# Results of two head pairs turned later, own banks for the last piece, twelve warming products

## The chip, the cores and the metric

The kernel runs on one core of a Trainium2 chip. The metric is the device time of one execution in microseconds (us); lower is better. A kernel is judged by the median of several runs, and one further execution is recorded by the hardware profiler. TensorE (PE) multiplies into PSUM banks, VectorE (DVE) and ScalarE (ACT) read those banks and write the on-chip memory, GpSimd (POOL) fills constants, and SyncE (SP) issues most transfers. All weights are read from the chip's main memory during the run.

## The reference

A trunk of four layers over one sequence of 256 tokens, width 1024, in float32. Each layer is a token mixer and a squared-ReLU MLP, each behind an RMS norm and added to the residual stream. The mixers are, in order, differential attention, block-sparse attention, sliding-window attention, and differential attention again. Of the differential layer:

```python
qkv = h @ w_in
q, k, v = jnp.split(qkv, [DIFF_QK_WIDTH, 2 * DIFF_QK_WIDTH], axis=-1)
...
p = jax.nn.softmax(s, axis=-1)
p = p[:, :, 0] - lam * p[:, :, 1]
return jnp.einsum('bhqk,bkhe->bqhe', p.astype(v.dtype), v)
...
o = rms_norm(o, sub_g) * (1.0 - lambda_init)
return o.reshape(B, S, H * DIFF_V_DIM) @ w_out
```

It has 8 heads, each with a query and a key of two halves and a value 128 wide. The trunk ends in a last RMS norm:

```python
h = h + sqrelu_mlp(rms_norm(h, mlp_norm_g[i]), mlp_w_up[i], mlp_w_down[i])
return rms_norm(h, final_norm_g)
```

## The kernel before

**Numbers in two parts.** Every float32 product is made as three products of rounded parts: a high part, and a low part that holds the rest. Weights come in pieces of 128 x 2048 (`raw`), fetched by SP five pieces ahead. `stage` splits a piece: ScalarE writes `whi` (L80), VectorE writes `wlo` (L81), each in two halves, two pieces ahead of use; `whi` and `wlo` have three buffers each, so the L80 of a piece waits until TensorE has done with the piece three before. Activations are split the same way (`hg`, `oo`, `uu`).

**Order.** The text of the program is recorded in order, and a scheduler then moves independent instructions on each engine a little. Each engine works through its own queue.

**A differential layer** (`mixer_layer` with `mixer == 0`). Six projections of 512 columns follow each other, `order = (0, 1, "v", 2, "v", 3)`: four give queries and keys of two heads each, two give values. One projection is 48 products: 24 for the first 128 tokens, then 24 for the second (`proj`, L296, output `p_in`). Work of earlier heads is placed by hand between these products: `plan[2 * at]` runs between the two sets of 24, `plan[2 * at + 1]` behind the projection's evacuation (L586 for queries and keys, L581 for values, and the rotary embedding on VectorE, L304 to L309), and `plan[-1]` behind the last projection. The steps in a plan are:
- `QK(c)`: turn queries and keys of two heads (`p_qk`, L459) and split them.
- `SC(h)`: scores and softmax of head h (`p_s`, L271 to L273; L333, L336, L385).
- `TR(h)`: turn the weights of head h (`p_t`, L351) and evacuate them on ScalarE (`et`, L352).
- `AV(h)`: for odd h, multiply a pair of heads with the values (`p_av`, L357 to L359), take the norm of the result (L399 on ScalarE, L400 and the steps of `rsqrt` on VectorE) and write the scaled result `o` (L404 on VectorE).
- `OUT(g)`: turn the result of pair g, four transposes `p_o` (L409), and split it into `oo` (L411 on ScalarE, then L412 on VectorE).

Then `out_proj_all` multiplies with the output weights in four quarters g, one piece each (`p_d`, L271 to L273). Quarter g uses pair g's result. In the last quarter each block is added to the residual stream and split for the next norm (`into`: L622, L228, L229).

PSUM has eight banks of 512 columns in two rings of four: `acc` for `p_in`, `p_d` and `p_last`, and `wk` for the rest.

**The end** (`down_out`, last layer). The last down projection is made in two column pieces c of 512, for two sets of 128 tokens t, into banks `p_last`. `close` adds a bank to the residual (L702, VectorE) and sums its squares (L704, ScalarE); `finish` makes the factor of the last norm with short steps on VectorE (L710 to L717), scales the rows (L719 on ScalarE, L722 on VectorE) and sends them out (L720, L723). For the last piece and the last tokens (c = 1, t = 1) the second half of the sum is made 256 columns at a time: 12 products and `close` for the first 256, then 12 products in the other half of the same bank and `close`.

**The start.** `WARM` products of 128 x 128 ones (`p_warm`, L133) run on TensorE while the first data comes.

Of the kernel before, what the change touches and what calls it, by code (L numbers as in the profile page):

```python
# [11 lines left out]
F32 = mybir.dt.float32  # L12
F32R = mybir.dt.float32r
I32 = mybir.dt.int32
AF = mybir.ActivationFunctionType
OP = mybir.AluOpType
AX = mybir.AxisListType

P = 128
# [8 lines left out]
NEG = -1.0e38  # L28
LOOK = 2
FAR = 5  # L30
WARM = 11
RAW = 4


# [5 lines left out]
def trunk(ctx: ExitStack, tc: tile.TileContext, xT, gains, lams, swa_row, fng, weights, out):  # L40
# [8 lines left out]
    def bank(tag, name):  # L49
        return ps.tile([P, 512], F32, tag=tag, name=name, bufs=4)  # L50
# [427 lines left out]
    def mixer_layer(i, n):  # L478
        mixer, slot = i % 3, i // 3
        r = norm_factor(n)  # L480
        parts = []
# [43 lines left out]
        else:  # L525
# [43 lines left out]
                    [(TR, 4), (QK, 3), (OUT, 1), (SC, 6)], [(TR, 5), (SC, 7)],  # L569
                    [(AV, 4), (TR, 6), (AV, 5), (TR, 7), (AV, 6), (OUT, 2), (AV, 7), (OUT, 3)]]  # L570
            if mixer == 0:
                plan[8:] = [[(AV, 2), (QK, 2), (OUT, 0), (SC, 4)], [(AV, 3), (SC, 5)], [(TR, 4), (AV, 4), (OUT, 1)],
                            [(TR, 5), (AV, 5)],
                            [(QK, 3), (SC, 6), (SC, 7), (OUT, 2), (TR, 6), (AV, 6), (TR, 7), (AV, 7), (OUT, 3)]]
            for at, c in enumerate(order):
                p = proj(n, (512, 2), at == 0, [lambda do=do, x=x: do(x) for do, x in plan[2 * at]])
                if i == 0 and at == 0:
# [11 lines left out]
                    do(x)  # L589
            for do, x in plan[-1]:  # L590
                do(x)
            return parts
        for do in first + second:
            do()
        for _ in range(3):
            step()
        line.clear()
        return parts

# [22 lines left out]
        if b:  # L624
            norm_sum(n, j)

    def out_proj_all(parts, n):

        banks = [bank("acc", f"p_d{j}") for j in range(4)]
        for g in range(4):  # L630
            hi, lo = (r3(2)(x) for x in take())
            for d in range(8):
                p = banks[d // 2][:, S * (d % 2):S * (d % 2) + S]
                w = slice(P * d, P * d + P)
                for a in range(2):
                    x = parts[2 * g + a]
                    mm3(p, hi[:, a, w], lo[:, a, w], x[:, 0], x[:, 1], g + a + d % 2 == 0, g + a == 4,
                        skip_group_check=True)
                if g == 3:
                    into(n, d, p, None, True)  # L640

    def out_proj(parts, n):

        banks = [bank("acc", f"p_d{j}") for j in range(4)]
        two = [[r3(4)(x) for x in take()] for _ in range(2)]
        order = [(k, d) for k in range(6) for d in range(4)] + [(k, d) for d in range(4) for k in (6, 7)]
        for k, d in order:
            hi, lo = (x[:, k % 4, P * d:P * d + P] for x in two[k // 4])
            block_step(banks[d], hi, lo, parts[k], k == 0, k == 7)
            if k == 7:  # L650
                into(n, d, banks[d], None)
        for j in range(2):
            hi, lo = (r3(8)(x) for x in take())
            for b in range(2):
                p = bank("acc", f"p_e{b}")
                for k in range(8):
                    block_step(p, hi[:, k, P * b:P * b + P], lo[:, k, P * b:P * b + P], parts[k], k == 0, k == 7)
                into(n, 4 + 2 * j + b, p, None)
# [32 lines left out]
    def down_out(us, res, factor):  # L691

        grow = sb.tile([P, D], F32, tag="raw", name="grow", bufs=RAW)
        nc.sync.dma_start(grow, bcast(fng, D))
        ss = cst.tile([P, 4, NT], F32, name="fss")
        x = cst.tile([P, 2, NT], F32, name="fx")
        r = cst.tile([P, NT], F32, name="fr")

        def close(t, bank, c, part, first, width):

            y = res[t][:, 512 * c + first:512 * c + first + width]
            V.scalar_tensor_tensor(y, bank[:, first:first + width], factor[:, t:t + 1], y, op0=OP.mult, op1=OP.add)  # L702
            sq = sb.tile([P, 512], F32, tag="relu", name="sq")
            A.activation(sq[:, :width], y, AF.Square, accum_out=ss[:, part, t:t + 1])  # L704

        def finish(t, halves):

            o = slice(t, t + 1)
            last = x[:, 1, o]
            V.scalar_tensor_tensor(last, ss[:, halves, o], 0.5 / D, x[:, 0, o], op0=OP.mult, op1=OP.add)  # L710
            y, w = r[:, o], tiny.tile([P, 1], F32, tag="nw", name="nw", bufs=6)

            V.tensor_scalar(y.bitcast(I32), last.bitcast(I32), -0.5, 1597463007.0 - 2.0 ** 22 - 2.0 ** 31,
                            op0=OP.mult, op1=OP.add)
            for _ in range(3):
                V.scalar_tensor_tensor(w, y, y, last, op0=OP.mult, op1=OP.mult)
                V.scalar_tensor_tensor(y, w, 1.5, y, op0=OP.subtract, op1=OP.mult)  # L717
            rows = slice(P * t, P * t + P)
            A.activation(res[t][:, :512], res[t][:, :512], AF.Copy, scale=y)  # L719
            nc.scalar.dma_start(out[rows, :512], res[t][:, :512])  # L720
            for z in (slice(512, 768), slice(768, 1024)):
                V.scalar_tensor_tensor(res[t][:, z], res[t][:, z], y, grow[:, z], op0=OP.mult, op1=OP.mult)  # L722
                nc.sync.dma_start(out[rows, z], res[t][:, z])  # L723

        def sofar(t, parts):
            o = slice(t, t + 1)
            V.tensor_scalar(x[:, 0, o], ss[:, 0, o], 0.5 / D, 0.5 * EPS, op0=OP.mult, op1=OP.add)
            for j in parts:
                V.scalar_tensor_tensor(x[:, 0, o], ss[:, j, o], 0.5 / D, x[:, 0, o], op0=OP.mult, op1=OP.add)

        for c in range(2):
            banks = [bank("acc", "p_last") for _ in range(NT)]
            parts = []

            def last(t, ks, cols=slice(0, 512)):
                for q, k in ks:
                    hi, lo = parts[q]
                    u, s = us[4 * q + k], slice(P * t, P * t + P)
                    mm3(banks[t][:, cols], u[:, 0, s], u[:, 1, s], hi[:, k, cols], lo[:, k, cols],
                        q + k == 0, q + k == 10, skip_group_check=True)  # L740

            for q in range(8):
                parts.append([r3(4)(x) for x in take()])
                if q < 6:
                    for k in range(4):
                        for t in range(NT):
                            last(t, [(q, k)])
            ends = [(q, k) for q in (6, 7) for k in range(4)]
            last(0, ends)
            close(0, banks[0], c, c, 0, 512)  # L750
            if c == 0:
                last(1, ends)
                close(1, banks[1], 0, 0, 0, 512)
                for t in range(NT):
                    y = res[t][:, :512]
                    V.tensor_tensor(y, y, grow[:, :512], op=OP.mult)
                    sofar(t, [])
            else:
                finish(0, 1)
                last(1, ends[:4])  # L760
                for h in range(2):
                    last(1, ends[4:], slice(256 * h, 256 * h + 256))
                    close(1, banks[1], 1, 1 + h, 256 * h, 256)
                    if h == 0:
                        sofar(1, [1])
                finish(1, 2)
# [7 lines left out]
    for j in range(4):  # L774
        norm_sum(n, j)
    for i in range(DEPTH):
        parts = mixer_layer(i, n)
        n = new_norm(gv[:, 1, i, :])
        (out_proj if i % 3 == 1 else out_proj_all)(parts, n)
        held = {}  # L780

        def then(g):
            if i + 1 < DEPTH:
                if g == 1:
                    x = mean_row(n)
                    held["row"] = sb.tile([P, S], F32, tag="row", name="row", bufs=1)
                    V.reciprocal(held["row"], x)
            elif g == 1:
                held["factor"] = cst.tile([P, NT], F32, name="factor")
                V.reciprocal(held["factor"], mean_square(n))  # L790

                held["res"] = [room(16 + t, [P, D], f"res{t}") for t in range(NT)]
                for j in range(4):
                    p = bank("acc", "p_res")
                    for t in range(NT):
                        for b in range(2):
                            T.transpose(p[:, S * t + P * b:S * t + P * b + P],
                                        hT[j][:, S * b + P * t:S * b + P * t + P], ident)
                    for t in range(NT):
                        A.activation(held["res"][t][:, S * j:S * j + S], p[:, S * t:S * t + S], AF.Copy)  # L800

        us = up_proj(n, then)
        if i + 1 < DEPTH:
            n = new_norm(gv[:, 0, i + 1, :])
            down_proj(us, n, held["row"])
        else:
            down_out(us, held["res"], held["factor"])
# [78 lines left out]
```

## Time and profile before

| what | value |
|---|---|
| median of 3 runs | 1155.39 us (1154.45 to 1156.26) |
| profiled execution, its own time | 1154.87 us |
| its span, first to last instruction | 1152.8 us |
| granted TensorE clock, mean | 0.998 |
| transfers | 198.66 MB, mean 172 GB/s |
| p_o (L409) | 32 transposes in 8 groups |
| L411, ScalarE | 8 times, mean 681 ns |
| L412, VectorE | 8 times, mean 743 ns |
| p_warm (L133) | 22 records for 11 products |

A float32 transpose or warming product shows as one or two records of TensorE. A start-to-start distance on TensorE is surer than an end, since the ends of pipelined products are modelled. The page's engine shares are means over stages; what one wait is worth is read in its place in the timeline.

### The profile page before, as it was taken

The page shows a single profiled execution, that of the slowest core. Times are in us where ns is not written, and L with a number is a line of the kernel's source. Part 1 is how long each engine was busy: PE and PEld are TensorE (multiplying, and loading weights), DVE is VectorE, ACT ScalarE, POOL GpSimd, SP SyncE. Part 2 cuts the span into 40 slices and gives each one's busy share as a digit, 9 for nine tenths or more (in the row PEclk, how much of TensorE's full clock was granted, in tenths as well). Part 3 has the DMA queues.
Part 4 walks back from the last instruction along what each step waited for, and adds up shares of the span by engine and source line. Part 5 has one row for each costly group of instructions (what it writes and reads, how often), then busy time and mean ns, then how long its engine had stood idle before and what let it go on. Part 6 is the DMA issues. An engine that isn't in the chain of part 4 may idle for free.

```text
span 1152.8 us, 17102 instructions
## 1 busy us (share of the span) xinstructions
PE 1140.4 (99%) x6558; PEld 986.6 (86%) x6558; DVE 824.3 (72%) x1631; ACT 671.6 (58%) x1239; POOL 11.4 (1%) x39
## 2 busy tenths in 40 slices
PE   9999999999999999999999999999999999999997
PEld 7789888888887888888898888888888889888886
DVE  8978977656666698775568787775567788777453
ACT  6866655544476765654447866654447676665342
POOL 1000000000000000000000000000000000000000
PEclk9999999999999999999999999999999999999999
DMA  8543455555544355555564246555553434554551
GB/s 327 194 146 119 160 200 193 199 190 183 183 146 145 116 178 193 200 192 183 185 209 142 74 147 206 195 184 186 184 201 129 152 136 155 194 199 166 186 179 36
DMA packets 30608, 198.66 MB, mean 172 GB/s; under 512 B 3520, under 2 KB 5184, under 8 KB 7360
## 3 DMA queue, kind: packets, MB, share of 16 engines
q1 hardware_dynamic: 30240, 197.06, 49.6%
q8 instruction: 51, 0.84, 0.3%
q10 hardware_dynamic: 288, 0.52, 0.1%
q14 instruction: 29, 0.24, 0.1%
HBM read 196.52 MB, written 1.05 MB: 171 GB/s over the span
## 4 chain that ended last, share of the span: by engine, by line
PE 92%; DVE 3%; ACT 2%; DMA 2%; issue 1%; SPq 0%; DVEq 0%; ACTq 0%
PE p_up L603 20%; PE p_in L296 16%; PE p_down L603 15%; PE p_up L604 10%; PE p_down L604 8%; PE p_last L271 2%; PE p_last L273 2%; PE p_last L272 2%; PE p_d L273 2%; PE p_d L271 2%; DMA raw<-in_weights 2%; PE p_d L272 2%; PE p_av L434 1%; PE p_t L351 1%; PE p_s L271 1%; PE p_qk L459 1%
## 5 line engine op out<-in xcount | busy, mean ns | idle before, releaser
L81 DVE TENSOR_TENSOR wlo<-raw,whi 128x1024 fp32r<-128x1024 f32 (+1 forms) x374 | 447.1, 1209 | 202.9 <-ACT whi L80 201.9
L80 ACT ACTIVATE whi<-raw 128x1024 fp32r<-128x1024 f32 (+1 forms) x374 | 384.7, 1045 | 210.1 <-issue 111.1
L603 PE MATMUL p_up<-hg,whi 128*128 128x512 f32 x1024 | 356.9, 393 | 0.5 <-DVE hg L229 0.2
L604 PE MATMUL p_up<-hg,wlo 128*128 128x256 f32 x1024 | 284.9, 279 | 0.0
L603 PE MATMUL p_down<-uu,whi 128*128 128x512 f32 x768 | 266.4, 392 | 0.0
L603 PEld LDWEIGHTS p_up<-hg,whi 128*128 128x128 f32 x1024 | 191.5, 187 | 43.3 <-DVE hg L229 0.7
L604 PE MATMUL p_down<-uu,wlo 128*128 128x256 f32 x768 | 214.3, 279 | 0.0
L296 PE MATMUL p_in<-whi,hg 128*128 128x512 f32 (+1 forms) x736 | 212.9, 372 | 0.1
L604 PEld LDWEIGHTS p_up<-hg,wlo 128*128 128x128 f32 x1024 | 193.2, 189 | 0.5
L603 PEld LDWEIGHTS p_down<-uu,whi 128*128 128x128 f32 x768 | 143.7, 187 | 32.1
L296 PEld LDWEIGHTS p_in<-whi,hg 128*128 128x128 f32 x736 | 131.8, 188 | 24.7 <-issue 1.2
L604 PEld LDWEIGHTS p_down<-uu,wlo 128*128 128x128 f32 x768 | 144.8, 189 | 0.0
L296 PE MATMUL p_in<-wlo,hg 128*128 128x512 f32 (+1 forms) x368 | 130.3, 368 | 0.1
L676 ACT ACTIVATE uu<-u 128x512 fp32r<-128x512 f32 x64 | 40.5, 633 | 70.9 <-DVE u L674 70.9
L296 PEld LDWEIGHTS p_in<-wlo,hg 128*128 128x128 f32 x368 | 68.8, 188 | 12.1 <-DVE wlo L81 1.3
L609 ACT ACTIVATE cross<-p_up 128x256 f32<-128x256 f32 x128 | 48.1, 376 | 39.4 <-PE p_up L604 34.0
L228 ACT ACTIVATE hg<-hT,gn 128x256 fp32r<-128x256 f32 x64 | 31.6, 503 | 65.6 <-DVE hT L622 65.1
L336 ACT ACTIVATE e<-ns,nm 128x128 f32<-128x128 f32 (+1 forms) x128 | 56.8, 447 | 10.3 <-DVE nm L333 10.0
L677 DVE TENSOR_TENSOR uu<-u,uu 128x512 fp32r<-128x512 f32 x64 | 44.2, 691 | 21.5 <-ACT uu L676 21.5
L271 PE MATMUL p_d<-oo,whi 128*128 128x256 f32 x192 | 56.2, 293 | 0.0
L272 PE MATMUL p_d<-oo,whi 128*128 128x256 f32 x192 | 55.1, 287 | 0.0
L273 PE MATMUL p_d<-oo,wlo 128*128 128x256 f32 x192 | 54.7, 288 | 0.0
(182 smaller groups left out, 1262.1 us busy)
## 6 DMA issues: line engine op xcount, KB each, us to landing
raw<-in_weights SPq DMA_DIRECT2D x181, 1024.0 KB, 4.8
raw<-in_weights SPq DMA_DIRECT2D x8, 256.0 KB, 4.6
raw<-in_weights SPq DMA_DIRECT2D x4, 512.0 KB, 7.6
hT<-in_xT SPq DMA_DIRECT2D x8, 128.0 KB, 4.5
bias<-in_swa_row SPq DMA_DIRECT2D x1, 512.0 KB, 3.6
grow<-in_fng SPq DMA_DIRECT2D x1, 512.0 KB, 3.5
out<-res SPq DMA_DIRECT2D x4, 128.0 KB, 2.1
out<-res ACTq DMA_DIRECT2D x2, 256.0 KB, 2.2
```

The costliest lines, as they stand in the source:

```text
L80: A.activation(hi[:, s], raw[:, s], AF.Copy)
L81: V.tensor_tensor(lo[:, s], raw[:, s], f(hi[:, s]), op=OP.subtract)
L271: T.matmul(out, lh, rh, start=start, stop=False, **kw)
L272: T.matmul(out, lh, rl, start=False, stop=False, **kw)
L273: T.matmul(out, ll, rh, start=False, stop=stop, **kw)
L296: T.matmul(out[t], n.both[k // 2][:, k % 2, x, P * t:P * t + P], r3(kb)(parts[k // kb][w])[:, k % kb, :], start=fresh, stop=k == 7 and x + ...
L336: A.activation(e[:, s], ns[:, s], AF.Exp, bias=nm[:, t:t + 1], scale=-1.0, accum_out=l[:, t:t + 1])
L603: T.matmul(r3(2)(p), hi, x, start=start, stop=False, skip_group_check=True)
L604: T.matmul(p[:, :S], lo, x[:, 0], start=False, stop=stop, skip_group_check=True)
L609: A.activation(cross, p[:, S:], AF.Copy)
L676: A.activation(both[:, :, 0], r3(2)(u), AF.Copy)
L677: V.tensor_tensor(both[:, :, 1], r3(2)(u), f(both[:, :, 0]), op=OP.subtract)
```

## The change

`OUT(1)` moves from the middle of the last projection to behind it, ahead of `TR(5)`. `OUT(3)` leaves the plan and is handed to `out_proj_all` as `rest`, which calls it in the third quarter ahead of block 4. The other mixers hand over an empty step. In `down_out`, the second half of the last sum goes into banks of its own: the first half is closed by a 512-wide L702 without squares, and each 256 columns get a fresh bank. `WARM` becomes 12.

```diff
-WARM = 11
+WARM = 12
...
-                plan[8:] = [[(AV, 2), (QK, 2), (OUT, 0), (SC, 4)], [(AV, 3), (SC, 5)], [(TR, 4), (AV, 4), (OUT, 1)],
-                            [(TR, 5), (AV, 5)],
-                            [(QK, 3), (SC, 6), (SC, 7), (OUT, 2), (TR, 6), (AV, 6), (TR, 7), (AV, 7), (OUT, 3)]]
+                plan[8:] = [[(AV, 2), (QK, 2), (OUT, 0), (SC, 4)], [(AV, 3), (SC, 5)], [(TR, 4), (AV, 4)],
+                            [(OUT, 1), (TR, 5), (AV, 5)],
+                            [(QK, 3), (SC, 6), (SC, 7), (OUT, 2), (TR, 6), (AV, 6), (TR, 7), (AV, 7)]]
...
-            return parts
+            return parts, (lambda: OUT(3))
...
-    def out_proj_all(parts, n):
+    def out_proj_all(parts, n, rest):
...
             for d in range(8):
+                if (g, d) == (2, 4):
+                    rest()
...
-        def close(t, bank, c, part, first, width):
+        def close(t, p, c, part, first=0):
+            width = p.shape[-1]
             y = res[t][:, 512 * c + first:512 * c + first + width]
-            V.scalar_tensor_tensor(y, bank[:, first:first + width], factor[:, t:t + 1], y, op0=OP.mult, op1=OP.add)
-            sq = sb.tile([P, 512], F32, tag="relu", name="sq")
-            A.activation(sq[:, :width], y, AF.Square, accum_out=ss[:, part, t:t + 1])
+            V.scalar_tensor_tensor(y, p, factor[:, t:t + 1], y, op0=OP.mult, op1=OP.add)
+            if part is not None:
+                sq = sb.tile([P, 512], F32, tag="relu", name="sq")
+                A.activation(sq[:, :width], y, AF.Square, accum_out=ss[:, part, t:t + 1])
...
                 last(1, ends[:4])
+                close(1, banks[1], 1, None)
                 for h in range(2):
-                    last(1, ends[4:], slice(256 * h, 256 * h + 256))
-                    close(1, banks[1], 1, 1 + h, 256 * h, 256)
+                    p = bank("acc", "p_last")[:, :256]
+                    last(1, ends[4:], p, 256 * h, True)
+                    close(1, p, 1, 1 + h, 256 * h)
                     if h == 0:
                         sofar(1, [1])
```

More of the change, by code (lines that the diff above doesn't have):

```diff
@@ L597, in mixer_layer @@
         line.clear()
-        return parts
+        return parts, lambda: None
     def block_step(p, hi, lo, x, start, stop):
@@ L640, in out_proj_all, with out_proj @@
                     into(n, d, p, None, True)
-    def out_proj(parts, n):
+    def out_proj(parts, n, rest):
         banks = [bank("acc", f"p_d{j}") for j in range(4)]
@@ L733, in down_out, with last @@
             parts = []
-            def last(t, ks, cols=slice(0, 512)):
+            def last(t, ks, p=None, first=0, alone=False):
+                p = banks[t] if p is None else p
+                cols = slice(first, first + p.shape[-1])
                 for q, k in ks:
@@ L738, in last @@
                     u, s = us[4 * q + k], slice(P * t, P * t + P)
-                    mm3(banks[t][:, cols], u[:, 0, s], u[:, 1, s], hi[:, k, cols], lo[:, k, cols],
-                        q + k == 0, q + k == 10, skip_group_check=True)
+                    mm3(p, u[:, 0, s], u[:, 1, s], hi[:, k, cols], lo[:, k, cols],
+                        (q, k) == (ks[0] if alone else (0, 0)), (q, k) == ks[-1] and k == 3 and q > 5,
+                        skip_group_check=True)
             for q in range(8):
@@ L749, in down_out @@
             last(0, ends)
-            close(0, banks[0], c, c, 0, 512)
+            close(0, banks[0], c, c)
             if c == 0:
                 last(1, ends)
-                close(1, banks[1], 0, 0, 0, 512)
+                close(1, banks[1], 0, 0)
                 for t in range(NT):
@@ L776, in trunk @@
     for i in range(DEPTH):
-        parts = mixer_layer(i, n)
+        parts, rest = mixer_layer(i, n)
         n = new_norm(gv[:, 1, i, :])
-        (out_proj if i % 3 == 1 else out_proj_all)(parts, n)
+        (out_proj if i % 3 == 1 else out_proj_all)(parts, n, rest)
         held = {}
```

## The prediction

> **What bounds the kernel now.** I read the busy shares of the page first, then the chain that ended last, then the list of waits of TensorE alone, and last the timeline around the three places that the change touches. Columns of a timeline row: start in us, duration in us, engine, line, operation, output<-inputs, shape, count, and in brackets the idle time before it with what ended it.
>
> ```profile
> PE 1140.4 (99%) x6558; PEld 986.6 (86%) x6558; DVE 824.3 (72%) x1631; ACT 671.6 (58%) x1239; POOL 11.4 (1%) x39
> ...
> PE 92%; DVE 3%; ACT 2%; DMA 2%; issue 1%; SPq 0%; DVEq 0%; ACTq 0%
> ```
> ```profile
> PE p_o L409 <- DVE o L404: 1.5, 4, 0.5
> ...
> PE p_last L271 <- DVE res L702: 0.6, 1, 0.6
> ```
>
> TensorE is busy for 99% of the span and carries 92% of the last chain. So an edit on another engine is worth nothing unless it closes a hole in TensorE's stream or shortens what follows its last product. The waits name exactly two kinds of hole that this change aims at: four waits of the transposes p_o for the VectorE result o, and one of p_last for L702. The list counts idle time after modelled ends, so I size each hole from starts instead.
>
> **The second pair's result, OUT(1).** First diff layer; the second has the same rows 843.5 us later.
>
> ```profile
> 84.45 0.39 PE L296 MATMUL p_in<-wlo,hg 128*128 128x512 f32 x1
> ...
> 85.08 0.63 PE L409 MATMUL p_o<-ident,o 128*128 128x128 f32 x4 [0.24 <-DVE o L404]
> ...
> 85.46 0.70 PE L296 MATMUL p_in<-whi,hg 128*128 128x512 f32 x2
> ...
> 85.74 0.69 ACT L411 ACTIVATE oo<-p_o,gn 128x512 fp32r<-128x512 f32 x1 [1.28 <-PE p_o L409]
> ...
> 87.36 1.06 ACT L80 ACTIVATE whi<-raw 128x1024 fp32r<-128x1024 f32 x1 [0.93 <-PE p_in L296]
> ```
> ```profile
> 89.67 0.39 PE L296 MATMUL p_in<-whi,hg 128*128 128x512 f32 x1
> ...
> 89.90 0.49 PE L351 MATMUL p_t<-ident,e 128*128 128x128 f32 x3
> 90.10 0.69 ACT L586 ACTIVATE qk<-p_in,nr 128x512 f32<-128x512 f32 x1 [0.72 <-PE p_in L296]
> ...
> 90.68 0.48 ACT L352 ACTIVATE et<-p_t 128x384 f32<-128x384 f32 x1
> ...
> 90.81 0.36 PE L271 MATMUL p_d<-oo,whi 128*128 128x256 f32 x1
> ...
> 91.22 0.30 PEld L357 LDWEIGHTS p_av<-v,et 128*128 128x128 f32 x2 [0.24 <-ACT et L352]
> ...
> 91.68 0.42 DVE L309 TENSOR_TENSOR qk<-ropea,ropeb 128x256 f32<-128x256 f32 x1
> ```
> ```profile
> 92.23 1.04 PE L459 MATMUL p_qk<-ident,qk 128*128 128x128 f32 x8
> ```
> ```profile
> 928.62 0.63 PE L409 MATMUL p_o<-ident,o 128*128 128x128 f32 x4 [0.24 <-DVE o L404]
> ```
>
> One p_in product takes 0.23 us from start to start (89.67 to 89.90). From 84.45 to 85.08 pass 0.63, so the hole is 0.40. The built order of the changed kernel (which instruction follows which on each engine, without times) puts the four transposes 19 products later, behind the last product of the projection and ahead of p_t; o is long ready there. Without hole and transposes the next product comes at 84.45 + 0.23 = 84.68 instead of 85.46: the rest of the projection runs 0.78 earlier, its last product at 88.89. The transposes start at 89.12 and take their 0.38 (85.08 to 85.46), p_t starts at 89.50, and the first p_d 0.91 later (89.90 to 90.81), at 90.41.
>
> The new danger is on ScalarE. L411 now stands between the L586 that empties the projection and the L352 that the second half of p_av waits for, and p_av already waited for L352 before (0.24). L586 moves with the projection to 89.32. L411 follows 0.58 later (90.10 to 90.68) at 89.90; the transposes are out at 89.12 + 0.63, in time. L411 lasts 0.69, so L352 starts by 90.59 at the latest, about 90.5 if the next instruction overlaps it as L352 overlaps L586. It ends near 90.98 and p_av starts 0.06 later, as it did (90.68 + 0.48 to 91.22): 91.04. TensorE's own slot would be about 90.73 (two p_d now stand ahead of it, 0.20 and 0.12), so a wait of some 0.3 stays. Against 91.22 that is 0.18 earlier, and one p_d more, worth 0.12, is already done: **0.30 us per layer**.
>
> The same queue rule holds on VectorE: L412 (0.74, a row below) now stands ahead of the rotary sum L309. That makes L309 start at 91.68 - 0.78 + 0.74 = 91.64 at the latest and end at 92.06. p_qk has its slot 1.01 after p_av (91.22 to 92.23), at 92.05: nothing, or 0.05. The pair of L80 ahead of L586 is released by p_in (87.36), so it moves with the projection and does not hold L586.
>
> Ends for this term: best the whole hole, 0.40. Worst, L352 moves back by all of L411 and none of the 0.78 counts: 91.22 + 0.69 - 0.12, a loss of 0.57. I take 0.30, since each of its starts hangs on a TensorE row that does move.
>
> [...]
>
> **The last pair's result, OUT(3).** It moves from ahead of the output projection into its third quarter.
>
> ```profile
> 109.86 0.28 PE L271 MATMUL p_d<-oo,whi 128*128 128x256 f32 x1
> 109.98 0.28 PE L272 MATMUL p_d<-oo,whi 128*128 128x256 f32 x1
> 110.78 0.63 PE L409 MATMUL p_o<-ident,o 128*128 128x128 f32 x4 [0.52 <-DVE o L404]
> 111.16 0.36 PE L273 MATMUL p_d<-oo,wlo 128*128 128x256 f32 x1
> ```
> ```profile
> 111.49 0.67 ACT L411 ACTIVATE oo<-p_o,gn 128x512 fp32r<-128x512 f32 x1
> 116.47 2.01 ACT L80 ACTIVATE whi<-raw 128x1024 fp32r<-128x1024 f32 x2 [4.31 <-PE p_d L272]
> ```
> ```profile
> 112.95 0.74 DVE L412 SCALAR_TENSOR_TENSOR oo<-p_o,gn,oo 128x512 fp32r<-128x512 f32 x1
> ```
> ```profile
> 954.31 0.63 PE L409 MATMUL p_o<-ident,o 128*128 128x128 f32 x4 [0.52 <-DVE o L404]
> ```
>
> p_d products follow each other every 0.12; 0.80 pass before p_o, so the hole is 0.68. The built order shows 19 more p_d ahead of the transposes, 2.3 us, so o is there. A change of kind costs TensorE a little even without a wait; I leave 0.08 of the hole for it: **0.60 per layer**, ends 0.50 and 0.68. What is late next: the last quarter needs both halves of this result, 24 products (2.9 us) after the transposes end. From the start of p_o: 0.71 to L411 (110.78 to 111.49), 0.67, and 0.74 for L412, together 2.12, against 0.38 + 2.88 = 3.26. Cover 1.1 us, if L411 is ahead of the L80 pair, as the built order has it. The four transposes and their two evacuations are the same instructions as before, and neither SP's nor GpSimd's queue is passed.
>
> **The last piece.** The second 256 columns get a bank of their own, and a 512-wide L702 without a square closes the first half of the sum.
>
> ```profile
> 1141.46 0.39 PE L273 MATMUL p_last<-whi,uu 128*128 128x512 f32 x1
> ...
> 1142.24 0.16 DVE L717 SCALAR_TENSOR_TENSOR fr<-nw,fr 128x1 f32<-128x1 f32 x1
> ...
> 1142.43 0.88 DVE L722 SCALAR_TENSOR_TENSOR res<-res,fr,grow 128x256 f32<-128x256 f32 x2
> ...
> 1143.00 0.28 PE L273 MATMUL p_last<-whi,uu 128*128 128x256 f32 x1
> ...
> 1143.85 0.39 PE L271 MATMUL p_last<-whi,uu 128*128 128x256 f32 x1 [0.58 <-DVE res L702]
> ...
> 1145.27 0.28 PE L273 MATMUL p_last<-whi,uu 128*128 128x256 f32 x1
> 1145.58 0.48 DVE L702 SCALAR_TENSOR_TENSOR res<-p_last,factor,res 128x256 f32<-128x256 f32 x1 [1.05 <-PE p_last L273]
> ```
> ```profile
> 1139.17 0.75 DVE L702 SCALAR_TENSOR_TENSOR res<-p_last,factor,res 128x512 f32<-128x512 f32 x1 [7.43 <-PE p_last L273]
> ```
>
> Without the wait the second half's first product starts at 1143.00 + 0.12 and its last 11 steps of 0.12 later, at 1144.44 instead of 1145.27: 0.83 earlier. The new L702 (0.75) stands in VectorE's queue ahead of the final L717 of the first 128 rows. Its data is there (1141.46 + 0.39 = 1141.85), so it runs from 1142.24 and pushes L717, the L722 pair and its two output DMAs back 0.75: the pair ends at 1143.31 + 0.75 = 1144.06. The first 256-wide L702 (0.48) then runs to 1144.54 and VectorE is free 0.2 before the last L702, at 1144.44 + 0.28 + 0.03 = 1144.75. So those 0.75 lie beside TensorE's last products. After that the chain to the last DMA is the same. **0.83 us**; ends 0.5, if the 0.75 shows in part, and 0.83.
>
> **The twelfth warming product.**
>
> ```profile
> 1.00 4.58 PE L133 MATMUL p_warm<-ones 128*128 128x128 f32 x22 [1.00 <-POOL ones L124]
> ...
> 5.68 0.30 PEld L296 LDWEIGHTS p_in<-whi,hg 128*128 128x128 f32 x2 [0.29 <-ACT hg L228]
> ...
> 6.40 0.30 PEld L296 LDWEIGHTS p_in<-whi,hg 128*128 128x128 f32 x2 [0.43 <-DVE hg L229]
> ```
>
> One product is two records; 22 take 4.58, so two more take at most 0.42. The first real product waits for ScalarE's hg at 5.68 with 0.29 idle, the next pair again with 0.43 idle. These waits hide it: 0, at worst 0.13 (0.42 - 0.29) and then eaten by the next wait.
>
> **Sum.** 2 × 0.30 + 2 × 0.60 + 0.83 + 0 = 2.63 us. The profiled execution took 1154.87 us (span 1152.8, 2.07 around it) and would take 1152.24. The median of the three runs, 1155.39, lies 0.52 above it and becomes 1152.76, predicted 1152.8. With the low ends except the improbable loss (0 for OUT(1), 0.50, 0.5, -0.13) the gain is 1.4, with the high ends (0.40, 0.68, 0.83) 3.0.
>
> **The rivals.** First, the wait of OUT(1) only changes its name: p_av's wait for L352 grows as p_o's wait goes. It decides if L352 starts 0.3 us later than I place it, for instance because ScalarE is still in an L80 when the projection ends. For it: p_av waits there already. Against: L80 moves with p_in. Gain 2 × 0.60 + 0.83 = 2.03, time 1153.4.
>
> Second, the slower one: OUT(3) comes too late for the last quarter. Place: L411 behind the L80 pair at 116.47 rather than ahead of it. That pair waits for the end of the third quarter, would run from 115.87 to 117.88, and L411 and L412 to 119.29, where the last quarter's low half is wanted at about 115.7: 3.6 lost in each layer where 0.60 was gained. It decides as soon as the result is over 1.1 us later than above. For it: the pair is the next thing in that queue. Against: the built order. Time 1155.39 + 7.2 - 0.60 - 0.83 - 1.20 = 1160.0.
>
> Third, the change doesn't reach TensorE's order because the scheduler had already moved these transposes. The built order shows all four at new places, so I give this nothing.
>
> **How the numbers follow.** A difference under 0.2% (2.3 us, below 1153.1) is about what a measurement of this kernel can't tell from none; the three runs spread over 1.8 us. My forecast clears that bound by only 0.3 us, so its chance is 0.62, the first rival and other partial gains 0.29, the second and what else makes it slower 0.09. Of these come faster 0.62, same 0.29, slower 0.09. The range goes from the high ends of the terms with the runs' scatter below them, 1151.6, past the first rival to a gain that scatter nearly hides, 1154.9.
>
> **What would show it.** Right: p_o gone from TensorE's waits, p_av's wait on L352 still about 0.2 to 0.3 in each diff layer, no wait at p_last, the last p_last product 2.6 us earlier. Wrong: p_av waiting over 0.5, p_d waiting for L411 or L412 at the start of the last quarter, or the last 256-wide L702 waiting in VectorE's queue instead of for TensorE.

## The result

| | median | range | profiled execution, span |
|---|---|---|---|
| before | 1154.9 us (7 runs) | 1154.45 to 1156.26 | 1154.87, 1152.8 |
| after | 1151.68 us (7 runs) | 1151.44 to 1151.98 | 1151.98, 1149.9 |

The ratio is 0.9972, 95% interval 0.9962 to 0.9982. The change saves 3.2 us, 0.28%, where 2.63 us was forecast; the time lies inside the range, 0.08 above its lower end.

The page of the kernel after, busy shares and the chain that ended last, and then TensorE's whole list of waits (us in total, times, longest):

```profile
PE 1139.2 (99%) x6560; PEld 988.0 (86%) x6560; DVE 824.6 (72%) x1632; ACT 671.1 (58%) x1239; POOL 11.4 (1%) x39
...
PE 95%; DVE 2%; DMA 1%; ACT 1%; issue 0%; SPq 0%; DVEq 0%
```
```profile
PE p_warm L133 <- POOL ones L124: 1.0, 1, 1.0
PE p_qk L459 <- DVE qk L309: 0.7, 1, 0.7
PE p_s L271 <- issue: 0.6, 1, 0.6
PE p_in L296 <- DVE wlo L81: 0.3, 1, 0.3
PE p_up L603 <- DVE hg L229: 0.2, 1, 0.2
```

Both kinds of hole that the change aims at are gone: no p_o, no p_last. The last p_last product starts 2.87 us earlier (1145.27 before). TensorE now carries 95% of the last chain instead of 92%. The p_in wait of 0.3 is new but belongs to the start, where the first weights land at different moments: the first L80, which waits for them, starts at 4.59 in the kernel before and at 4.37 in after. It must be kept apart from the change, so I measure stages from start to start on TensorE. Rows of the kernel before (first p_o of the first differential layer, its first p_up, then p_sum and p_up at the two ends of the last layer's mixer), and the same of after:

```profile
68.27 0.60 PE L409 MATMUL p_o<-ident,o 128*128 128x128 f32 x4
...
120.45 0.50 PE L603 MATMUL p_up<-hg,whi 128*128 128x512 f32 x1
...
859.12 0.60 PE L249 MATMUL p_sum<-ones,acc 128*128 128x128 f32 x3
...
963.99 0.50 PE L603 MATMUL p_up<-hg,whi 128*128 128x512 f32 x1
```
```profile
68.55 0.60 PE L409 MATMUL p_o<-ident,o 128*128 128x128 f32 x4
...
119.60 0.50 PE L603 MATMUL p_up<-hg,whi 128*128 128x512 f32 x1
...
858.24 0.71 PE L249 MATMUL p_sum<-ones,acc 128*128 128x128 f32 x4
...
961.95 0.50 PE L603 MATMUL p_up<-hg,whi 128*128 128x512 f32 x1
...
1142.40 0.28 PE L273 MATMUL p_last<-whi,uu 128*128 128x256 f32 x1
```

Differences of these starts (worked out before rounding, so that a row can be 0.01 off), for these two kernels and for the parts of the change run alone (experiments below):

| kernel | first layer, p_o to p_up | last layer, p_sum to p_up | p_up to last p_last | last p_last to end of span |
|---|---|---|---|---|
| before | 52.18 | 104.86 | 181.28 | 7.49 |
| after | 51.05 | 103.71 | 180.45 | 7.48 |
| OUT(1) alone | 51.73 | 104.45 | 181.28 | 7.50 |
| OUT(3) alone | 51.47 | 104.22 | 181.28 | 7.49 |
| last piece alone | 52.19 | 104.86 | 180.45 | 7.49 |
| warming alone | 52.17 | 104.91 | 181.27 | 7.49 |

The change takes 1.13 and 1.15 us out of the two mixers and 0.83 out of the end: 3.11. The two profiled executions differ by only 2.89, because the one of after began its first p_o 0.28 later (68.55 against 68.27).

**OUT(1) after the change.** Timeline of the kernel after, where the last projection ends:

```profile
89.05 0.39 PE L296 MATMUL p_in<-whi,hg 128*128 128x512 f32 x1
...
89.28 0.60 PE L409 MATMUL p_o<-ident,o 128*128 128x128 f32 x4
...
89.71 0.49 PE L351 MATMUL p_t<-ident,e 128*128 128x128 f32 x3
...
90.06 0.68 ACT L411 ACTIVATE oo<-p_o,gn 128x512 fp32r<-128x512 f32 x1
...
90.63 0.49 ACT L352 ACTIVATE et<-p_t 128x384 f32<-128x384 f32 x1
...
91.17 0.30 PEld L357 LDWEIGHTS p_av<-v,et 128*128 128x128 f32 x2 [0.27 <-ACT et L352]
...
91.60 0.42 DVE L309 TENSOR_TENSOR qk<-ropea,ropeb 128x256 f32<-128x256 f32 x1
...
92.18 0.49 PE L459 MATMUL p_qk<-ident,qk 128*128 128x128 f32 x3
```

L352 starts as L411 ends, 0.57 after L411's start, and p_av waits for it (0.27, and again 0.27 in the last layer): the wait that the prediction kept is there. Whether a ready L352 could pass L411 is not shown: p_t is out at 90.20, when L411 has run since 90.06, so L352 had nothing to pass. On VectorE L309 starts at 91.60, as L412 (from 90.94, 0.75 long) ends, though its last input is out at 91.02 (L307). p_qk follows the product ahead of it (92.06) without a wait, as L309 is done at 92.02.

**OUT(3) after the change.** Timeline of the kernel after, third quarter of the output projection:

```profile
112.10 0.28 PE L273 MATMUL p_d<-oo,wlo 128*128 128x256 f32 x1
112.22 0.60 PE L409 MATMUL p_o<-ident,o 128*128 128x128 f32 x4
...
112.58 0.36 PE L271 MATMUL p_d<-oo,whi 128*128 128x256 f32 x1
...
112.78 0.28 PE L272 MATMUL p_d<-oo,whi 128*128 128x256 f32 x1
...
112.86 0.69 ACT L411 ACTIVATE oo<-p_o,gn 128x512 fp32r<-128x512 f32 x1 [1.43 <-PE p_o L409]
...
113.58 0.75 DVE L412 SCALAR_TENSOR_TENSOR oo<-p_o,gn,oo 128x512 fp32r<-128x512 f32 x1 [0.71 <-ACT oo L411]
```

p_o starts 0.12 after the p_d ahead of it, the plain step of such products, so nothing of the hole is left. The result is ready at 114.33; its low half is wanted by the 26th product after p_o, at about 112.58 + 0.08 + 25 × 0.12 = 115.66. The cover is 1.3 us.

**The end after the change.** Lines below L701 moved down by three to four: L705 and L721 are the L702 and L717 of before.

```profile
1140.09 0.74 DVE L705 SCALAR_TENSOR_TENSOR res<-p_last,factor,res 128x512 f32<-128x512 f32 x1
...
1140.75 0.15 DVE L721 SCALAR_TENSOR_TENSOR fr<-nw,fr 128x1 f32<-128x1 f32 x1
...
1141.73 0.48 DVE L705 SCALAR_TENSOR_TENSOR res<-p_last,factor,res 128x256 f32<-128x256 f32 x1
...
1142.71 0.48 DVE L705 SCALAR_TENSOR_TENSOR res<-p_last,factor,res 128x256 f32<-128x256 f32 x1 [0.50 <-PE p_last L273]
```

The last L705 waits 0.50 for TensorE, not for its queue. The added 512-wide L705 therefore lies wholly beside TensorE's last products.

### The profile page after: what moved, and what is told of

Read it like the earlier page. It is cut to its first block, busy times and chain, and to the rows that moved or that the text cites. A ratio compares the mean times of both kernels' runs of the same rounds, so it can differ in the third digit from the quotient of the medians.

```text
span 1149.9 us, 17106 instructions
## 1 busy us (share of the span) xinstructions
PE 1139.2 (99%) x6560; PEld 988.0 (86%) x6560; DVE 824.6 (72%) x1632; ACT 671.1 (58%) x1239; POOL 11.4 (1%) x39
## 4 chain that ended last, share of the span: by engine, by line
PE 95%; DVE 2%; DMA 1%; ACT 1%; issue 0%; SPq 0%; DVEq 0%
PE p_up L603 20%; PE p_in L296 18%; PE p_down L603 15%; PE p_up L604 11%; PE p_down L604 8%; PE p_last L273 3%; PE p_last L271 3%; PE p_last L272 3%; PE p_d L273 2%; PE p_d L271 2%; PE p_d L272 2%; PE p_t L351 1%; PE p_av L434 1%; PE p_s L271 1%; PE p_qk L459 1%; DVE wlo L81 1%
## 5 line engine op out<-in xcount | busy, mean ns | idle before, releaser
L81 DVE TENSOR_TENSOR wlo<-raw,whi 128x1024 fp32r<-128x1024 f32 (+1 forms) x374 | 447.3, 1209 | 205.5 <-ACT whi L80 204.5
L80 ACT ACTIVATE whi<-raw 128x1024 fp32r<-128x1024 f32 (+1 forms) x374 | 384.7, 1045 | 208.2 <-issue 111.1
L271 PE MATMUL p_d<-oo,whi 128*128 128x256 f32 x192 | 55.8, 291 | 0.0
L272 PE MATMUL p_d<-oo,whi 128*128 128x256 f32 x192 | 55.2, 288 | 0.0
```

What stands on the lines that cost most here:

```text
L80: A.activation(hi[:, s], raw[:, s], AF.Copy)
L81: V.tensor_tensor(lo[:, s], raw[:, s], f(hi[:, s]), op=OP.subtract)
L271: T.matmul(out, lh, rh, start=start, stop=False, **kw)
L272: T.matmul(out, lh, rl, start=False, stop=False, **kw)
```

## The experiments

**The four parts, each alone.** Each is the kernel before with one part of the change (the third was made from the kernel after by taking the other parts back).

OUT(1) alone:

```diff
-[(TR, 4), (AV, 4), (OUT, 1)], [(TR, 5), (AV, 5)],
+[(TR, 4), (AV, 4)], [(OUT, 1), (TR, 5), (AV, 5)],
```

> The kernel before with OUT(1) alone moved behind the last projection. Theory (the whole hole before p_o goes, one change between transposes and products goes with it, and p_av's wait on L352 stays at about 0.24): 0.45 us in each differential layer, 0.9 us in all, time ratio 0.9992. The prediction's own term would give 0.30 a layer, 0.6 us, ratio 0.9995. Rival (the wait only changes its name to p_av): under 0.2 us in all and a p_av wait over 0.5 us.

OUT(3) alone:

```diff
-[(QK, 3), ..., (TR, 7), (AV, 7), (OUT, 3)]]
+[(QK, 3), ..., (TR, 7), (AV, 7)]]
...
+                if (g, d) == (2, 4):
+                    rest()
```

> The kernel before with OUT(3) alone moved into the third quarter of the output projection. Theory: the whole hole of 0.68 us in each differential layer, 1.36 us, ratio 0.9988; no wait of p_d for L411 or L412. The prediction's term: 0.60 a layer, 1.2 us. Rival (the result is late for the last quarter): a wait at the first p_d of the last quarter and a gain under 1 us.

The last piece alone:

```diff
                 last(1, ends[:4])
+                close(1, banks[1], 1, None)
                 for h in range(2):
-                    last(1, ends[4:], slice(256 * h, 256 * h + 256))
-                    close(1, banks[1], 1, 1 + h, 256 * h, 256)
+                    p = bank("acc", "p_last")[:, :256]
+                    last(1, ends[4:], p, 256 * h, True)
+                    close(1, p, 1, 1 + h, 256 * h)
```

> The kernel before with the last piece's own banks alone. Theory: the last p_last product 0.83 us earlier, all of it kept up to the last transfer, ratio 0.9993. Rival (the extra 512-wide evacuation holds up VectorE's queue): the last 256-wide evacuation starts later than 0.03 us after TensorE's last product ends, and the gain is 0.5 us or less.

The twelfth product alone:

```diff
-WARM = 11
+WARM = 12
```

> The kernel before with twelve warming products alone. Theory: the extra product lies beside the wait for the first data, 0.0 us, ratio 1.0000 within 0.0005, and the runs scatter as those of the kernel before. Rival (the twelfth keeps the clock up or steadies the start): 0.3 us or more faster and a narrower scatter of the runs, which would account for the 0.3 us by which the medians differ more than the two profiles.

Measured beside the kernel before on the same chip (1154.99 us, 33 runs):

| part | median (11 runs each) | ratio and interval | saved, medians | saved, stages of the profile |
|---|---|---|---|---|
| OUT(1) | 1154.15 | 0.9993 [0.9984, 1.0002] | 0.84 | 0.45 + 0.41 |
| OUT(3) | 1153.69 | 0.9989 [0.9980, 0.9998] | 1.30 | 0.71 + 0.64 |
| last piece | 1154.18 | 0.9993 [0.9984, 1.0001] | 0.81 | 0.83 |
| warming | 1155.09 | 0.9998 [0.9989, 1.0007] | -0.10 | 0 |

One part by itself is at the edge of what the times resolve; only OUT(3) has an interval below one. The stage lengths resolve each, and the medians agree with them within 0.1 us. The parts add up: 2.95 by the medians without the warming (2.85 with it), 3.04 by the stages, against 3.2 and 3.11 for the whole. That they disturb one another does not show.

**After once more, as a measure for its neighbours.** The changed kernel, unaltered.

> The changed kernel once more, to compare the following with on one chip and to tell whether the gain of 3.2 us between the medians is more than the 3.1 us that the stages show (1.13 and 1.15 in the two differential layers, 0.83 at the end). Theory (stages alone, the rest is when the first weights land): 1151.9 us against 1155.0, ratio 0.9973, with p_o's first start between 68.2 and 69.6 us in any profile. Rival (the parts help each other): 1151.5 or less and a stage that is shorter than in the runs of single parts.

1152.04 us (1151.30 to 1153.01) against 1154.87 of before; ratio 0.9975 [0.9967, 0.9984]; stages 51.04, 103.74, 180.44. This is what the stages alone give. Only the band for the first p_o was too narrow: one of the profiles below has 67.98.

**Does the warming matter at all?** One product instead of twelve, in the changed kernel.

```diff
-    for _ in range(WARM):
+    for _ in range(1):
```

> The changed kernel with one warming product instead of twelve. Theory (the granted clock rises a fixed time after the first products and the first data hides most): the first projection runs at the lower clock until about 9 to 12 us, 0.5 to 2 us slower than the changed kernel. Rival (waits for data hide all of it): equal within 0.2 us, and the twelfth product can then not matter either.

1152.46 us (1151.82 to 1153.29), 0.42 above the run before, just under the 0.5 to 2 us that was expected. TensorE's waits of this kernel, and its first products in two stretches, followed by the same stretches of after (columns: length, busy time and count of TensorE, its weight loads, VectorE, ScalarE, GpSimd, granted clock, share of the transfer engines, GB/s):

```profile
PE p_in L296 <- ACT hg L228: 3.9, 1, 3.9
```
```profile
8.00:11.40 3.40, 3.40 (x9) 2.64 (x8) 2.77 (x6) 2.96 (x7) 0.00 (x0) 1.00 1.03 369
11.40:14.00 2.60, 2.60 (x13) 2.13 (x12) 2.60 (x6) 2.60 (x7) 0.00 (x0) 1.00 0.80 261
```
```profile
8.00:11.40 3.40, 3.40 (x15) 2.48 (x15) 3.05 (x8) 3.40 (x8) 0.00 (x0) 1.00 0.90 318
11.40:14.00 2.60, 2.60 (x13) 2.11 (x12) 2.60 (x6) 2.60 (x6) 0.00 (x0) 1.00 1.07 389
```

From 8.0 to 11.4 us it gets through 9 products where after gets through 15; from 11.4 on both do 13. The trace's record of the granted clock begins only with full clock, at 11.40 us here and at 4.45 in after, so the view says 1.00 ahead of it too; the products say otherwise: they follow each other by 0.43 us here until then and by 0.23 behind it. So the clock is full earlier with twelve warming products (from 4.45) than with one (from 11.40). What that is worth is less clear: the first p_o comes at 69.51, against 68.55 and 68.43 in two profiles of the changed kernel, but the profile of the last piece alone, with eleven products, has 69.57. The medians differ by 0.42 and the ranges overlap, so neither 0.4 us nor the rival's nothing is excluded. Nor is the rise at a fixed time after the first product: that starts at 1.00 in before and in after, the full clock at 4.93 and 4.45, and before, in which it is later, has the earlier p_o (68.27 against 68.55). The step from eleven to twelve buys nothing that shows.

**How much cover OUT(3) has.** Its call three blocks, 18 products, later.

```diff
-                if (g, d) == (2, 4):
+                if (g, d) == (2, 7):
```

> The changed kernel with OUT(3) three blocks later, ahead of block 7 of the third quarter, so that 6 products instead of 24 lie between its transposes and the last quarter. Theory (the cover was 1.1 us, 18 products are 2.16): the last quarter waits, some 0.5 to 1.1 us a layer after the scheduler puts four first products together, 1 to 2 us slower than the changed kernel. Rival (the cover is larger than worked out, nothing waits): equal to the changed kernel within 0.2 us.

1153.27 us (1152.81 to 1154.92), 1.2 above the unaltered one beside it. Timeline, last quarter:

```profile
113.80 0.60 PE L409 MATMUL p_o<-ident,o 128*128 128x128 f32 x4
...
114.44 0.69 ACT L411 ACTIVATE oo<-p_o,gn 128x512 fp32r<-128x512 f32 x1 [3.59 <-PE p_o L409]
...
114.83 0.28 PE L273 MATMUL p_d<-oo,wlo 128*128 128x256 f32 x1
...
115.16 0.75 DVE L412 SCALAR_TENSOR_TENSOR oo<-p_o,gn,oo 128x512 fp32r<-128x512 f32 x1 [2.87 <-ACT oo L411]
115.18 0.73 PE L271 MATMUL p_d<-oo,whi 128*128 128x256 f32 x4
115.96 0.38 PE L272 MATMUL p_d<-oo,whi 128*128 128x256 f32 x1
...
118.34 0.28 PE L273 MATMUL p_d<-oo,wlo 128*128 128x256 f32 x1
118.87 0.38 PE L271 MATMUL p_d<-oo,whi 128*128 128x256 f32 x1 [0.25 <-DVE hT L622]
```

The first p_d of the last quarter starts at 115.18, as L411 ends (114.44 + 0.69 = 115.13), 0.35 after the product ahead of it instead of 0.12; L272 starts at 115.96, as L412 ends (115.91). From start to start that is 0.24 and 0.22 lost in this layer. A third wait follows: the p_d at 118.87 waits for L622, which adds the first block to the residual stream. L622 starts at 118.41, behind two roundings of weights (L81, from 116.13) that stand behind it in after, where it starts at 116.46. That costs 0.41, so 0.87 in this layer and 1.7 in two. From the first p_o to the last p_last this profile is 1.6 longer than that of after, and the medians say 1.2. 18 products are 2.16 us, 0.8 more than the cover of 1.33; the first two waits come to half of that, since four L271 products, which need only the high half, were drawn ahead of the first L272. So OUT(3) can come too late, as the slower rival says, but the place that the change chose is clear of it.

**Can p_av's wait be taken away too?** OUT(1) between TR(5) and AV(5), so that L352 stands ahead of L411 on ScalarE.

```diff
-                            [(OUT, 1), (TR, 5), (AV, 5)],
+                            [(TR, 5), (OUT, 1), (AV, 5)],
```

> The changed kernel with TR(5) ahead of OUT(1), so that L352 stands ahead of L411 in ScalarE's queue and L309 ahead of L412 in VectorE's. Theory (ScalarE's order sets p_av's wait, but the next wait is close behind): p_av's wait of 0.24 goes, p_qk then waits about 0.3 for the rotary sum since no p_d is left between, and the net is 0 to 0.15 us a layer faster than the changed kernel, 0.3 us at most. Rival (p_av's wait is all that is left there): 0.25 to 0.3 us a layer, 0.5 to 0.6 in all. If the order on ScalarE were not what sets it, p_av would wait as before.

1157.34 us (1155.45 to 1160.13), ratio 1.0023 [1.0014, 1.0032]: 5.3 slower than the unaltered one beside it, where at most 0.5 to 0.6 faster was expected. At the place itself the theory held: p_av has no wait, p_qk waits 0.19 for L309, and counted from the first p_o it starts 0.65 earlier with four p_d (0.48) fewer done, a gain of 0.17. The loss is 25 us further on. TensorE's waits of this kernel, its timeline at the last quarter, and two stretches around it, followed by one from the last layer (columns as above):

```profile
PE p_d L271 <- ACT oo L411: 1.6, 2, 0.8
PE p_o L409 <- DVE o L404: 1.2, 2, 0.6
...
PE p_d L272 <- DVE oo L412: 0.4, 2, 0.2
```
```profile
114.79 0.28 PE L273 MATMUL p_d<-oo,wlo 128*128 128x256 f32 x1
115.65 0.63 PE L409 MATMUL p_o<-ident,o 128*128 128x128 f32 x4 [0.57 <-DVE o L404]
117.06 0.74 PE L271 MATMUL p_d<-oo,whi 128*128 128x256 f32 x4 [0.78 <-ACT oo L411]
```
```profile
114.80:118.20 3.40, 1.82 (x12) 1.20 (x11) 2.80 (x4) 2.69 (x3) 0.00 (x0) 1.00 0.65 272
118.20:121.60 3.40, 3.40 (x17) 3.40 (x18) 2.25 (x4) 1.02 (x2) 0.00 (x0) 0.50 0.39 106
...
961.29:964.70 3.41, 2.19 (x15) 1.77 (x15) 2.82 (x4) 2.25 (x3) 0.00 (x0) 1.00 0.46 192
```

The scheduler answered the swap with another order for pair 7. It set 28 p_d products instead of 5 between the transposes of head 6 and those of head 7, and roundings of weights (L80, L81) between the steps of pair 7's norm, so L404 started on the last result at 114.81 instead of 109.91. p_o then stands right ahead of the last quarter, 48 products from the end instead of 72. This is what the prediction's slower rival feared, a result too late for the last quarter, though by another way (it had L411 behind the L80 pair, and 3.6 us a layer): from start to start 0.75, 1.00 and 0.40 us lost in each of the two layers, 4.3 in all. Then, in the first layer only, the granted clock is 0.50 from 118.2 to 121.6. The 17 steps from the first L272 on take 3.64 us there (118.03 to 121.67) and 2.17 in the last layer (963.88 to 966.05): 1.5 us more. Together that is 5.8, or 5.5 less the 0.17 won twice at the first place; the profile shows 5.4 from the first p_o to the last p_last (1079.22 against 1073.85).

**Is it the swap or pair 7?** OUT(1) behind TR(5) and AV(5). In the built order this leaves pair 7 as in after (72 products behind the last p_o).

```diff
-                            [(OUT, 1), (TR, 5), (AV, 5)],
+                            [(TR, 5), (AV, 5), (OUT, 1)],
```

> The changed kernel once more, as the measure for its neighbour in this comparison: 1151.7 to 1152.1 us by all theories, 2.8 to 3.3 below the kernel before.

> The changed kernel with OUT(1) behind TR(5) and AV(5) instead of ahead of them; order of the second part for the last pair as in the changed kernel (the transposes of pair 7 with few products between them, 54 products behind OUT(3)). In the run with OUT(1) between TR(5) and AV(5) the turn of OUT(1) cost nothing, p_av did not wait and p_qk started at 91.16 us instead of 92.07; that run lost its time only 25 us later, where pair 7 came 4.9 us late. Theory: the loss belongs to pair 7's late chain alone, so here the gain of the first place stays: p_qk starts 0.9 us earlier, with four products (0.48 us) fewer done before it, which is 0.4 us in each of two layers: 0.8 us below the changed kernel, 1151.1 us, with no p_d waiting for L411 or L412. Rival: OUT(1) behind the rotation makes its eviction late (two roundings of weights, 2.0 us, stand ahead of it on ScalarE), and a product of OUT(1) waits for it: 0.5 to 1.5 us above the changed kernel. Second rival: the wait for the rotation (p_qk for L309) takes the place, and the time is that of the changed kernel within 0.3 us.

The unaltered kernel took 1151.83 us (1151.18 to 1152.23; before 1154.98, ratio 0.9970 [0.9959, 0.9982]), this one 1152.19 (1151.90 to 1153.07; ratio 0.9975 [0.9965, 0.9985]). Its stages are 51.12 and 103.83 against 51.00 and 103.74: nothing lost to pair 7, nothing won either, which is the second rival. So TR(5) ahead of OUT(1) is not itself harmful; the late pair was. The expected gain of 0.4 per layer was in good part a slip: it compares starts of p_qk (91.16 and 92.07) in two profiles that had begun 0.25 apart (first p_o at 68.18 and 68.43). Counted from the first p_o, p_qk came 0.65 earlier in that run and 0.5 earlier here than in after, and the four products not yet done are worth 0.48.

```profile
90.42 0.27 PE L409 MATMUL p_o<-ident,o 128*128 128x128 f32 x1
90.74 0.49 PE L357 MATMUL p_av<-v,et 128*128 128x128 f32 x2
...
91.51 0.49 PE L409 MATMUL p_o<-ident,o 128*128 128x128 f32 x3
91.84 1.04 PE L459 MATMUL p_qk<-ident,qk 128*128 128x128 f32 x8
```

The scheduler drew one of the four transposes ahead of p_av, and even so p_av waits: 0.32 from p_o to p_av, where one transpose takes 0.11. No version tried beats after.

## Why the prediction was right

**What bounds the kernel** held. TensorE's holes were the whole gain: the stretch between the two mixers kept its length (859.12 - 120.45 = 738.67 before, 738.64 after), and the end of the span stayed 7.5 us behind the last product.

**OUT(1): mechanism right, size low.** 0.45 and 0.41 measured alone, 0.30 forecast. Both lie above the 0.40 that the prediction called the best end. The order came out as described, p_av's wait on L352 included. The mis-sized step is the p_av start: forecast 91.04, which on the profile of after, begun 0.28 later, would be 91.32; it came at 91.17. Of the 0.15, 0.12 is there already at the end of the projection: forecast 88.89, so 89.17, measured 89.05. Before, 18 steps from 85.46 to 89.67 took 4.21 us; 18 of 0.228 are 4.10. The missing 0.1 lies in the first of them. The first product behind the transposes starts 0.03 after the last transpose (85.43 to 85.46), where transposes follow each other by 0.11, and the next product comes 0.31 later: the two steps add up to the usual 0.11 and 0.23. So the start at 85.46 is 0.08 too early to measure by, and the prediction's 0.78 for hole and transposes was too small by that. From 84.45 (84.73 in after) to p_t stand the same products and transposes in both kernels; there the hole was worth 5.45 - 4.98 = 0.47. The expectation of the run with OUT(1) alone had the right size, 0.45, but put the difference down to a change of kind, which by these rows costs nothing.

**OUT(3): mechanism right, the 0.08 wrong.** 0.71 and 0.64 alone, mean 0.68, the whole hole; 0.60 forecast, with 0.08 left for a change of kind. As much lies between the first p_d behind the transposes and the others in the prediction's rows (0.36 and 0.28 long), but no run shows it as a cost: going from p_d to transposes costs nothing (112.10 to 112.22), and neither does leaving them (the last transpose starts at 112.55, the products behind it at 112.58 and 112.78: together 0.23, one transpose and one product). The cover was 1.3 where 1.1 was forecast, and the late version showed what becomes of it.

**The last piece: exact.** 0.83 forecast, 0.83 measured in each profile that has it. Only VectorE's margin was larger, 0.50 against 0.2. The 512-wide step began 0.1 earlier against the last product than I had placed it, and each following step starts some 0.08 before the one ahead of it ends (1140.09 + 0.74 to 1140.75), which I had added end to end.

**The twelfth product: right.** 0 forecast, -0.10 by medians with an interval on both sides of one, 0 by stages.

**The sum.** The misses, 0.26 on OUT(1) and 0.15 on OUT(3), have the same sign and make up the difference between 2.63 and 3.04. The forecast time, 1152.8, was 1.1 above the measured one, and for this there is a second reason: it started from 1155.39, the median of three runs, where seven gave 1154.90, so 0.5 of the 1.1 is scatter of the starting point and 0.6 the gain. Even the high ends, 3.0, would have ended at 1152.4; that 1151.68 lies inside the range is owed to the room left below them for scatter, and is in part luck. The first rival (the wait only changes its name) did not happen: p_av's wait went from 0.24 to 0.27, not over 0.5. Of the second (OUT(3) too late) nothing happened here, but two of the experiments brought its effect about. The third was excluded by the order alone.

## What to carry to other kernels

Move work that waits for another engine to a place where TensorE has other products ready, and size the gain by start-to-start distances over a stretch that ends on products of one kind; a hole filled with independent products was worth all of itself here. Before moving it, work out the cover from the moved step to the first product that needs its result, because the loss beyond the cover is steep: 1.7 us of waits in one experiment, 4.3 in another. Where a scheduler fills in the order, a swap of two neighbouring steps can move something 25 us away, so read the new order to the end of the stage before giving a price.

## What the runs showed of the hardware

**A clock that fell after short holes.** In the run with the late pair 7 the record of the granted clock has half clock from 118.19 to 121.61, 3.42 us, after a stretch of 3.4 us in which TensorE was 54% busy (1.82 of 3.40) and no hole was over 1.0 us. The last layer of the same run has the same three holes (0.75, 1.00 and 0.40 lost) and no fall. Nor does the busy share of a stretch alone order the cases: in after TensorE is 46% busy from 1141.09 to 1144.51 (1.58 of 3.42), and the clock stays full until 1147.92. What decides is not shown. The runs of the kernel with the late pair 7 spread over 4.7 us, those of after beside it over 1.7. Falls in some of the runs, at the 1.5 us worked out for the one seen, could do that. This is an estimate; the granted clock listed for each run fits it: 0.999 in its two fastest, 0.997 in its three slowest.

**No cost of changing kind.** The first product after a group of transposes starts 0.03 after the last of them and is followed by the next one 0.20 later instead of 0.12 (112.58 to 112.78 in after, 111.16 to 111.36 in before). This looks like a slow step, but the two add up to one transpose (0.11) and one product (0.12), in the groups of p_o before and after alike. A distance that ends on such a first product is 0.08 short in these rows.

**The start.** In twelve profiles the first p_o starts between 67.98 and 69.57 us. In the profile of the last piece alone, for example, p_in waits 0.8 for `whi` and 0.5 for `wlo`, neither of which stands among the waits of the kernel before. Differences below a microsecond are read from stage lengths here, not from two spans.
